# The last down group of the feed-forward parts: four column tiles instead of two, gone through token tile by token tile

## Chip, cores and metric

One core of a Trainium2 chip runs the whole program once. The metric is the device time of that execution in microseconds (us). Before the change the median of three runs is 1692.49 us (1692.39 to 1693.67).

## What is computed

Two layers of a block with 256 latent tokens (x) and 256 context tokens (ctx), 1024 wide. Each layer is: a feed-forward part, a mixer (two kinds of attention and a short convolution), a second feed-forward part. The last layer's second feed-forward part is made for the 256 latent tokens only, since only they are returned.

```python
def swiglu(u, wi, wo):
    g, up = jnp.split(u @ wi, 2, axis=-1)      # wi: 1024 x 5632
    return (jax.nn.silu(g) * up) @ wo          # wo: 2816 x 1024

h = post(h, swiglu(pre(h, m, 0, 0), ffn_wi[0], ffn_wo[0]), m, 0, 1, 0.5)
```

`pre` is an RMS norm with a scale and a shift per column, `post` adds the gated, normed result to the residual stream h. So there are four feed-forward parts: parts 1 (layer 0, first), 2 (layer 0, second) and 3 (layer 1, first) over 512 tokens, part 4 (layer 1, second) over 256.

## The kernel before

**Number format.** Every product of two matrices is made of three matmuls: both operands are split into a high and a low half (`a` and the weight slot `w` hold both; `Uh`/`Ul` are the halves of the normed tokens), and high x high, low x high and high x low are summed in PSUM. `mm` (line 79) issues them all, so the profile has one line for them; tiles and shapes tell them apart: `mm<-Uh,w` or `mm<-Ul,w` is an up matmul, `mm<-w,a` a down matmul, `mm<-w,Uh` one of a stage that goes token tile by token tile. The name ahead of the arrow (`at`, `mm`, `pv`) is only the PSUM bank's: six banks are handed out in the turn at, mm, at, mm, pv, mm.

**Weights.** `load_unit` (lines 86 to 95) brings one unit of 512 KB by DMA on the SP queue into a staging tile (two of them, three more in part 4), ScalarE casts it to the high half (line 93), VectorE subtracts to get the low half (line 94). A ring of eight slots holds the units. A slot is free again when the last matmul that reads it is done.

**A feed-forward part** (`ffn`). The 2816 inner columns are 22 column tiles f. `up` makes, for each f of a list, the gate and the up product (2 x 8 x 3 = 48 matmuls over the tokens of a segment), then `silu` (line 314, ScalarE), the product (315, VectorE), the high half (320, ScalarE) and the low half (321, VectorE) of `a[f]`. `down` multiplies a group of column tiles with wo: for each (t, hf) of a list of parts, t a token tile of 128 and hf a half of the 1024 output columns, 3 matmuls per f, all summed in one bank, which VectorE then adds to `y` (line 367; ScalarE copies the first group). `FGROUPS` says which column tiles are a group; ups are made one group ahead.

**The end of a part.** After the last group each (t, hf) has its sum of squares (line 208, ScalarE) and its gate product (370, VectorE); when hf is 1, `post(t)` makes the inverse root on GpSimd (line 99) and adds to H (274, VectorE, twice 512), and `after(t)` runs `pre(t)` for the next stage: two sums of squares of H (208), again an inverse root (104, 99), the scaled row `xn` (220, ScalarE), eight transposes on TensorE (225), scale and shift into `uf` (239 ScalarE, 241 VectorE), and the halves into the columns of tile t of `Uh` and `Ul` (243 ScalarE, 244 VectorE). `Uh`, `Ul`, `xn` and `uf` exist once. In part 4 `after` is the store.

The token order is t = 2, 3, 0, 1. In parts 1 to 3 the end is in pieces: the up of tiles 20 and 21 is made over tokens 256 to 511 before the down of group (16, 4), and over tokens 0 to 255 only after token tiles 2 and 3 have had their last down:

```python
down(20, 2, wu, [[(2, 0), (2, 1)], [(3, 0), (3, 1)]], False, True)
up([20, 21], wup, [(0, 8, 0, 256)], 0, 256)
down(20, 2, wu, [[(t, hf) for t in (0, 1) for hf in range(2)]], False, True)
```

so that the pre of tiles 2 and 3 runs beside the second up. The stage that follows begins with tile 2: the mixer (`token_block(2)`, after parts 1 and 3) and `up_first` of part 3 (after part 2) take eight units for tile 2, four and four, 24 matmuls of 512 columns for each four (in the mixer of the last layer the second 24 have 128 columns for tiles 2 and 3).

**Order.** Each engine's order of instructions is fixed ahead by a planner that plays the program with modelled times and takes what is ready, earlier work in the program first. Steps of the modulation vectors (`ada_step`, lines 151 to 164: one unit by DMA, then one or two multiply-reduces of 1024 on VectorE, line 162, whose product goes into `uf`) are hung behind the evictions of f = 3 to 19.

Of the kernel before, what the change touches and what calls it, by code (L numbers as in the profile page):

```python
# [16 lines left out]

D = 1024
NF = 22
FGROUPS = [(0, 4), (4, 4), (8, 4), (12, 4), (16, 4), (20, 2)]  # L20
EPS = 1e-6
NEG = -1e30

# [2 lines left out]
def tile_hybrid_block(ctx: ExitStack, tc: tile.TileContext, xin, c2, crow, w_ada, w_ada0, bcol, gcol, win, qkg, bias_in,  # L26
# [51 lines left out]
    def mm(out, lhsT, rhs, first, last):  # L78
        pe.matmul(out, lhsT=lhsT, rhs=rhs, start=first, stop=last)  # L79
# [6 lines left out]
    def load_unit(src):  # L86
        if more_stg:
            s = more_stg[0].tile([128, 1024], F32, name="stgx", tag="stgx", bufs=3)
        else:
            s = stg.tile([128, 1024], F32, name="stg", tag="stg")  # L90
        sp.dma_start(out=s, in_=src)
        w = next_slot()
        act.copy(w[:, 0], s)  # L93
        dve.tensor_tensor(out=w[:, 1], in0=s, in1=w[:, 0].bitcast(F32), op=ALU.subtract)  # L94
        return w
# [97 lines left out]
    def ada_to(ph, n):  # L193
        while ada_done[0] < min(n, len(ada_todo)):
            ada_todo[ada_done[0]](ph)
            ada_done[0] += 1

    def load_gate(l, mi, nv):
        G = work.tile([128, 2, 1024], F32, name="G", tag="G")
        dr = gates.pop(9 * l + mi)  # L200
        pool.dma_start(out=G[:, 0:nv].rearrange("p v c -> p (v c)"),
                       in_=bass.AP(tensor=dr.tensor, offset=dr.offset, ap=[[0, 128], [1, 1024 * nv]]))
        return G

    def sumsq(src, n):
        j = work.tile([128, 1024], BF16, name="junk", tag="junk")
        ss = small.tile([128, 1], F32, name="ss", tag="ss", bufs=12)
        act.activation(j[:, 0:n], src, AF.Square, accum_out=ss)  # L208
        return ss
# [60 lines left out]
    def post(t, yg, ss0, ss1):  # L270
        r = rsum(sum_eps(ss0, ss1))
        for i, y in enumerate(yg):
            h = H[t][:, 512 * i:512 * i + 512]
            dve.scalar_tensor_tensor(out=h, in0=y, scalar=r, in1=h, op0=ALU.mult, op1=ALU.add)
# [14 lines left out]
    def ffn(ph, l, i, U, tiles, after, ada_target, mode):  # L289
# [6 lines left out]
        def load_up(fs):  # L296
            return {(f, u): load_unit(wi[l, i, f, u]) for f in fs for u in range(2)}

        def up(fs, ws, segs, c0, n):
            pss = {(f, u): cur["mm"]() for f in fs for u in range(2)}  # L300
            for k0, nk, s0, sn in segs:
                for f in fs:
                    for u in range(2):
                        w = ws[f, u]
                        po = pss[f, u][:, s0 - c0:s0 - c0 + sn]
                        for kt in range(k0, k0 + nk):
                            wh = w[:, 0, 128 * kt:128 * kt + 128]
                            wl = w[:, 1, 128 * kt:128 * kt + 128]
                            mm(po, wh, U[0][:, kt, s0:s0 + sn], kt == 0, False)
                            mm(po, wh, U[1][:, kt, s0:s0 + sn], False, False)  # L310
                            mm(po, wl, U[0][:, kt, s0:s0 + sn], False, kt == 7)
            for f in fs:
                sg = ph.tile([128, 512], F32, name="sg", tag="sg")
                act.activation(sg[:, 0:n], pss[f, 0][:, 0:n], AF.Silu)
                dve.tensor_tensor(out=sg[:, 0:n], in0=pss[f, 1][:, 0:n], in1=sg[:, 0:n], op=ALU.mult)  # L315
                if f not in acts:
                    acts[f] = ph.tile([128, 2, n_c], F32R, name="a", tag="a", bufs=6)
                a = acts[f]
                c = slice(c0 - lo_c, c0 - lo_c + n)
                act.copy(a[:, 0, c], sg[:, 0:n])  # L320
                ins = dve.tensor_tensor(out=a[:, 1, c], in0=sg[:, 0:n], in1=a[:, 0, c].bitcast(F32), op=ALU.subtract)
                if f == 10:
                    n0 = len(nc.cur_bb.bb.instructions)
                    G.append(load_gate(l, mi, 1 if len(tiles) == 2 else 2))
                    tc.add_manual_dep(nc.cur_bb.bb.instructions[n0], ins.ins.name,
                                      mybir.DependencyInfo(mybir.DependencyClass.NoSync, mybir.DependencyReason.DATA),
                                      reason="gate late")
                if c0 == lo_c and 3 <= f < 20:
                    with tc.issue_after(ins.ins):
                        ada_to(ph, ada0 + (ada_target - ada0) * (f - 2) // 17)  # L330

        def up_all(fs, mode=""):
            if mode == "k":
                segs = [(2 * qd, 2, lo_c, n_c) for qd in range(4)]
            elif mode[0:3] == "tok":
                segs = [(0, 8, 256, 256), (0, 8, 0, 256)]
            else:
                segs = [(0, 8, lo_c, n_c)]
            up(fs, load_up(fs), segs, lo_c, n_c)

        def load_down(f0, nf, hf):
            return [load_unit(wo[l, i, (f0 + fp) // 2, hf]) for fp in range(0, nf, 2)]

        def down(f0, nf, wu, parts, first, last):
            for part in parts:
                ps = {x: cur["mm"]() for x in part}
                for f in range(nf):
                    for t, hf in part:
                        if hf not in wu:
                            wu[hf] = load_down(f0, nf, hf)  # L350
                        p = ps[t, hf]
                        c = 128 * t - lo_c
                        ah, al = acts[f0 + f][:, 0, c:c + 128], acts[f0 + f][:, 1, c:c + 128]
                        wh = wu[hf][f // 2][:, 0, 512 * (f % 2):512 * (f % 2) + 512]
                        wl = wu[hf][f // 2][:, 1, 512 * (f % 2):512 * (f % 2) + 512]
                        mm(p, ah, wh, f == 0, False)
                        mm(p, al, wh, False, False)
                        mm(p, ah, wl, False, f == nf - 1)
                for t, hf in part:
                    p = ps[t, hf]  # L360
                    if t not in ys:
                        ys[t] = ph.tile([128, 1024], F32, name="y", tag="y", bufs=len(tiles))
                    y = ys[t][:, 512 * hf:512 * hf + 512]
                    if first:
                        act.copy(y, p)
                    else:
                        dve.tensor_tensor(out=y, in0=p, in1=y, op=ALU.add)  # L367
                    if last:
                        sss[t, hf] = sumsq(y, 512)
                        dve.tensor_tensor(out=y, in0=y, in1=G[0][:, 0 if t < 2 else 1, 512 * hf:512 * hf + 512], op=ALU.mult)  # L370
                        if hf == 1:
                            post(t, [ys[t][:, 0:512], ys[t][:, 512:1024]], sss[t, 0], sss[t, 1])
                            after(t)
# [23 lines left out]
        else:  # L397
            up_all([0, 1, 2], mode)
            up_all([3])
        for g, (f0, nf) in enumerate(FGROUPS[:-1]):  # L400
            f1 = f0 + nf
            if f1 < 20:
                up_all([f1, f1 + 1])
            elif len(tiles) == 4:
                wup = load_up([20, 21])
                up([20, 21], wup, [(0, 8, 256, 256)], 256, 256)
            else:
                up_all([20, 21])
            down(f0, nf, {}, [[(t, hf)] for hf in range(2) for t in tiles], g == 0, False)
            if f1 < 20:  # L410
                up_all([f1 + 2, f1 + 3])
        wu = {}
        if len(tiles) == 4:
            down(20, 2, wu, [[(2, 0), (2, 1)], [(3, 0), (3, 1)]], False, True)
            up([20, 21], wup, [(0, 8, 0, 256)], 0, 256)
            down(20, 2, wu, [[(t, hf) for t in (0, 1) for hf in range(2)]], False, True)
        else:
            down(20, 2, wu, [[(t, hf)] for t in tiles for hf in range(2)], False, True)

    def mixer(ph, l, U, after):  # L420
        full = l == 0
# [278 lines left out]
    with phase("ffn") as ph:  # L700
        ffn(ph, 0, 0, U, order, after, 54, "k")
# [4 lines left out]
    with phase("ffn") as ph:  # L706
        ffn(ph, 0, 1, box2[0], order, after, 90, "tok1")
    box2, after = chain(1, 1)
    with phase("ffn") as ph:
        ffn(ph, 1, 0, box[0], order, after, 144, "tok2")  # L710
# [83 lines left out]
```

## Time and profile before

| | |
|---|---|
| median of three runs | 1692.49 us (1692.39 to 1693.67) |
| the profiled execution | 1692.87 us |
| its span (first to last instruction) | 1691.0 us |
| mean granted TensorE clock over the span | 0.997 |
| busy: TensorE matmul / weight load / VectorE / ScalarE / GpSimd | 98% / 83% / 68% / 43% / 3% |
| moved by DMA | 259.98 MB, mean 154 GB/s |

The profile is of one execution. It lies 0.38 us above the median of the runs, and 1.87 us of it are outside the span. PE is TensorE's matmuls, PEld its weight loads, DVE VectorE, ACT ScalarE, POOL GpSimd, SPq the queue that issues most DMAs. Since matmuls are pipelined, the duration of one is longer than the step from one to the next; steps are read from the starts or from the chain of waits, which lists each instruction with the time by which it carries the chain on.

### The profile page before, as it was taken

To read this page: it belongs to the slowest core of one execution; us is meant where nothing else is said; L and a number is where in the kernel's file an instruction comes from. 1 tells how busy PE (TensorE), PEld (TensorE's weight loads), DVE (VectorE), ACT (ScalarE), POOL (GpSimd) and SP (SyncE) were. 2 spreads that over 40 slices of the span, in tenths; PEclk is the share of its full clock that TensorE was granted. 3 is DMA by queue.
4 is the path that set the end of the run, shared out by engine and by line. 5 is a ranking of instruction groups with operands and counts; after the bars stand their busy time and mean duration, and the time that the engine had idled before them with its cause. 6 is when DMAs were issued, how large, how long until landed. Compare 5 with 4: busy or idle time off the path is not lost.

```text
span 1691.0 us, 23323 instructions
## 1 busy us (share of the span) xinstructions
PE 1662.5 (98%) x9012; PEld 1406.9 (83%) x9012; DVE 1146.9 (68%) x1917; ACT 720.4 (43%) x1247; POOL 46.9 (3%) x77
## 2 busy tenths in 40 slices
PE   6999999999999999999999999999999999999997
PEld 4888888888887789888888888888888889879997
DVE  3578787667766665476675566887785768865654
ACT  5432222227656683322222364322222557865442
POOL 1000000001100010000000000000000020000000
PEclk9999999999999999999999999999999999999999
DMA  8565555432121334454444134665563322456551
GB/s 322 200 226 197 174 200 189 160 112 106 63 75 51 94 125 162 149 193 145 161 163 148 64 137 155 216 204 189 167 215 125 106 94 101 138 172 215 181 193 64
DMA packets 73503, 259.98 MB, mean 154 GB/s; under 512 B 8440, under 2 KB 11728, under 8 KB 72496
## 3 DMA queue, kind: packets, MB, share of 16 engines
q1 hardware_dynamic: 72144, 252.81, 43.9%
q0 software_dynamic: 1248, 5.68, 1.0%
q8 instruction: 71, 1.16, 0.3%
q14 instruction: 40, 0.33, 0.1%
HBM read 257.37 MB, written 1.09 MB: 153 GB/s over the span
## 4 chain that ended last, share of the span: by engine, by line
PE 96%; DVE 1%; ACT 1%; DMA 1%; issue 0%; SPq 0%; POOL 0%; DVEq 0%; POOLq 0%; ACTq 0%
PE mm L79 52%; PE at L79 27%; PE pv L79 14%; PE ptr L590 2%; PE ptr L225 1%; DMA H<-in_xin_dram 0%; ACT junk L208 0%; DMA stg<-in_wi_tm_dram 0%; ACT w L93 0%; DMA bias<-in_bias_dram 0%; ACT xn L220 0%; DVE y L370 0%; DVE w L94 0%; PE ptr L469 0%; DVE y L367 0%
## 5 line engine op out<-in xcount | busy, mean ns | idle before, releaser
L79 PE MATMUL mm<-Uh,w 128*128 128x512 f32 (+1 forms) x1808 | 486.2, 348 | 0.0
L93 ACT CAST w<-stg 128x1024 fp32r<-128x1024 f32 x262 | 274.7, 1051 | 442.9 <-PE mm L79 392.2
L94 DVE TENSOR_TENSOR w<-stg,w 128x1024 fp32r<-128x1024 f32 x262 | 319.6, 1222 | 163.5 <-ACT w L93 162.5
L79 PEld LDWEIGHTS mm<-Uh,w 128*128 128x128 f32 x1808 | 319.2, 189 | 42.8 <-issue 0.6
L79 PE MATMUL mm<-Ul,w 128*128 128x512 f32 (+1 forms) x904 | 314.5, 348 | 0.0
L162 DVE CUSTOM_DVE_ANT_0 uf<-adas,CB 128x1024 f32<-128x1024 f32 x248 | 302.7, 1221 | 14.9 <-DMA adas<-in_w_ada_dram 11.1
L79 PE MATMUL at<-Uh,w 128*128 128x512 f32 (+1 forms) x960 | 254.1, 344 | 0.0
L79 PE MATMUL mm<-w,a 128*128 128x512 f32 x924 | 226.7, 389 | 0.0
L79 PEld LDWEIGHTS mm<-w,a 128*128 128x128 f32 x924 | 173.4, 188 | 35.9
L79 PEld LDWEIGHTS mm<-Ul,w 128*128 128x128 f32 x904 | 171.2, 189 | 21.1 <-issue 0.2
L79 PEld LDWEIGHTS at<-Uh,w 128*128 128x128 f32 x960 | 169.0, 190 | 22.0 <-issue 0.4
L79 PE MATMUL mm<-w,Uh 128*128 128x512 f32 (+1 forms) x544 | 171.1, 387 | 0.4 <-ACT w L93 0.4
L79 PE MATMUL at<-Ul,w 128*128 128x512 f32 (+1 forms) x480 | 165.4, 345 | 0.4 <-DVE Ul L267 0.4
L79 PE MATMUL at<-w,a 128*128 128x512 f32 x594 | 146.8, 390 | 0.9 <-ACT a L320 0.9
L79 PEld LDWEIGHTS at<-w,a 128*128 128x128 f32 x594 | 111.0, 188 | 24.3 <-ACT a L320 1.8
L79 PE MATMUL pv<-Uh,w 128*128 128x512 f32 (+1 forms) x464 | 127.6, 353 | 0.0
L79 PEld LDWEIGHTS mm<-w,Uh 128*128 128x128 f32 x544 | 100.4, 188 | 19.6 <-ACT w L93 0.7
L315 DVE TENSOR_TENSOR sg<-mm,sg 128x512 f32<-128x512 f32 (+1 forms) x86 | 51.3, 597 | 90.9 <-PE mm L79 85.0
L94 DVE TENSOR_TENSOR w<-stgx,w 128x1024 fp32r<-128x1024 f32 x58 | 71.0, 1224 | 52.5 <-ACT w L93 52.3
L79 PE MATMUL mm<-w,Ul 128*128 128x512 f32 (+1 forms) x272 | 105.2, 387 | 0.0
L79 PEld LDWEIGHTS at<-Ul,w 128*128 128x128 f32 x480 | 91.1, 190 | 11.8 <-DVE Ul L267 1.0
L79 PEld LDWEIGHTS pv<-Uh,w 128*128 128x128 f32 x464 | 82.7, 189 | 12.0
(161 smaller groups left out, 1709.8 us busy)
## 6 DMA issues: line engine op xcount, KB each, us to landing
adas<-in_w_ada_dram SPq DMA_DIRECT2D x144, 512.0 KB, 3.4
stg<-in_wi_dram SPq DMA_DIRECT2D x124, 512.0 KB, 4.0
stg<-in_wo_dram SPq DMA_DIRECT2D x66, 512.0 KB, 3.3
stg<-in_win_dram SPq DMA_DIRECT2D x40, 512.0 KB, 3.3
stgx<-in_wi_dram SPq DMA_DIRECT2D x36, 512.0 KB, 4.2
stgx<-in_wo_dram SPq DMA_DIRECT2D x22, 512.0 KB, 4.3
stg<-in_woa_dram SPq DMA_DIRECT2D x16, 512.0 KB, 3.3
stg<-in_wi_tm_dram SPq DMA_DIRECT2D x16, 512.0 KB, 3.3
```

The lines of the kernel that those rows point to most:

```text
L79: pe.matmul(out, lhsT=lhsT, rhs=rhs, start=first, stop=last)
L93: act.copy(w[:, 0], s)
L94: dve.tensor_tensor(out=w[:, 1], in0=s, in1=w[:, 0].bitcast(F32), op=ALU.subtract)
L162: dve.tensor_tensor_reduce(out=junk, in0=s, in1=CB[:, v], op0=ALU.mult, op1=ALU.add, scale=1.0, scalar=0.0, accum_out=ada_mc[m][:, v, cb:c ...
L225: pe.transpose(pt[:, b], xn[:, 128 * k:128 * k + 128], I)
L315: dve.tensor_tensor(out=sg[:, 0:n], in0=pss[f, 1][:, 0:n], in1=sg[:, 0:n], op=ALU.mult)
L590: pe.transpose(pt[:, b], P[:, 128 * b:128 * b + 128], I)
```

## The change

The groups become five of 4, 4, 4, 4, 2 and a last one of 4. The up of tiles 20 and 21 is made over all tokens, the last group (tiles 18 to 21) is gone through by token tile, and within one by half: (2,0), (2,1), (3,0), (3,1), (0,0), (0,1), (1,0), (1,1), or in part 4 (0,0), (0,1), (1,0), (1,1). The sequence at the end becomes: up 18, 19; down of group (16, 2); up 20, 21; down of group (18, 4).

```diff
-FGROUPS = [(0, 4), (4, 4), (8, 4), (12, 4), (16, 4), (20, 2)]
+FGROUPS = [(0, 4), (4, 4), (8, 4), (12, 4), (16, 2), (18, 4)]
...
         for g, (f0, nf) in enumerate(FGROUPS[:-1]):
             f1 = f0 + nf
-            if f1 < 20:
-                up_all([f1, f1 + 1])
-            elif len(tiles) == 4:
-                wup = load_up([20, 21])
-                up([20, 21], wup, [(0, 8, 256, 256)], 256, 256)
-            else:
-                up_all([20, 21])
+            up_all([f1, f1 + 1])
             down(f0, nf, {}, [[(t, hf)] for hf in range(2) for t in tiles], g == 0, False)
-            if f1 < 20:
+            if FGROUPS[g + 1][1] == 4:
                 up_all([f1 + 2, f1 + 3])
-        wu = {}
-        if len(tiles) == 4:
-            down(20, 2, wu, [[(2, 0), (2, 1)], [(3, 0), (3, 1)]], False, True)
-            up([20, 21], wup, [(0, 8, 0, 256)], 0, 256)
-            down(20, 2, wu, [[(t, hf) for t in (0, 1) for hf in range(2)]], False, True)
-        else:
-            down(20, 2, wu, [[(t, hf)] for t in tiles for hf in range(2)], False, True)
+        down(18, 4, {}, [[(t, hf)] for t in tiles for hf in range(2)], False, True)
```

## Rows read from the trace of the kernel before

**Rows 1.** The page: busy us (share of the span) xinstructions; chain of waits by engine.

```profile
PE 1662.5 (98%) x9012; PEld 1406.9 (83%) x9012; DVE 1146.9 (68%) x1917; ACT 720.4 (43%) x1247; POOL 46.9 (3%) x77
...
PE 96%; DVE 1%; ACT 1%; DMA 1%; issue 0%; SPq 0%; POOL 0%; DVEq 0%; POOLq 0%; ACTq 0%
```

**Rows 2.** PE's waits over the span: us in total, times, longest us.

```profile
PE ptr L225 <- ACT xn L220: 12.1, 4, 10.2
```

**Rows 3.** The chain of waits, end of part 1: start us, us, what.

```profile
334.86 5.44 PE mm L79 x24
340.30 2.87 PE at L79 x24
...
348.93 2.88 PE mm L79 x24
...
379.04 2.87 PE pv L79 x24
...
387.67 2.88 PE mm L79 x24
```

**Rows 4.** PE's waits in 978 to 981 us, then in 1348 to 1375 us.

```profile
PE at L79 <- ACT a L320: 0.9, 1, 0.9
...
PE ptr L225 <- ACT xn L220: 0.8, 1, 0.8
```

**Rows 5.** The timeline of PE, ACT and DVE, end of part 4: start us, us.

```profile
1680.81 1.52 PE L79 MATMUL mm<-w,a 128*128 128x512 f32 x6
...
1682.36 0.69 DVE L367 TENSOR_TENSOR y<-mm,y 128x512 f32<-128x512 f32 x1
...
1683.69 0.19 ACT L208 ACTIVATION_READ_ACCUMULATOR junk<-y 128x1 f32 x1
...
1683.57 1.41 DVE L274 SCALAR_TENSOR_TENSOR H<-y,rr,H 128x512 f32<-128x512 f32 x2
1684.89 0.68 DVE L370 TENSOR_TENSOR y<-y,G 128x512 f32<-128x512 f32 x1
1685.50 0.21 DVE L104 TENSOR_SCALAR sst<-ss 128x1 f32<-128x1 f32 x1
```

**Rows 6.** The page's groups: the modulation steps on VectorE.

```profile
L162 DVE CUSTOM_DVE_ANT_0 uf<-adas,CB 128x1024 f32<-128x1024 f32 x248 | 302.7, 1221 | 14.9 <-DMA adas<-in_w_ada_dram 11.1
```

**Rows 7.** The timeline, PE, ACT and DVE: eviction of a 512-token column tile, part 1.

```profile
329.25 0.39 PE L79 MATMUL pv<-Uh,w 128*128 128x512 f32 x1
...
329.45 1.06 ACT L93 CAST w<-stg 128x1024 fp32r<-128x1024 f32 x1 [3.90 <-PE mm L79]
330.41 0.62 ACT L320 CAST a<-sg 128x512 fp32r<-128x512 f32 x1
...
331.68 0.68 DVE L321 TENSOR_TENSOR a<-sg,a 128x512 fp32r<-128x512 f32 x1
```

**Rows 8.** The timeline, PE, ACT and DVE: tile 2's end, part 1, then part 2.

```profile
376.15 0.84 PE L79 MATMUL at<-w,a 128*128 128x512 f32 x3
...
386.70 1.15 ACT L220 ACTIVATE xn<-H,rr 128x1024 f32<-128x1024 f32 x1
387.91 1.05 ACT L93 CAST w<-stg 128x1024 fp32r<-128x1024 f32 x1
...
391.09 1.03 PE L225 MATMUL ptr<-I,xn 128*128 128x128 f32 x8
...
394.54 1.29 DVE L244 TENSOR_TENSOR Ul<-uf,Uh 128x512 fp32r<-128x512 f32 x2
...
960.27 0.84 PE L79 MATMUL at<-w,a 128*128 128x512 f32 x3
...
979.71 1.29 DVE L244 TENSOR_TENSOR Ul<-uf,Uh 128x512 fp32r<-128x512 f32 x2
```

**Rows 9.** ACT's timeline after part 1; the page's DMA issues (median us to landing).

```profile
398.41 1.04 ACT L93 CAST w<-stg 128x1024 fp32r<-128x1024 f32 x1
...
stg<-in_wi_tm_dram SPq DMA_DIRECT2D x16, 512.0 KB, 3.3
```

## The prediction, made before the changed kernel was run

> **What bounds the kernel now.** I read the page's busy times and chain first: PE is busy for 98% of the span and carries 96% of the chain of waits [rows 1]. Then PE's waits: the largest kind is 12.1 us, of which one wait at the start is 10.2 [rows 2]. So almost all the time is matmul steps issued back to back. The change can win by fewer or shorter matmul steps and by waits of PE that go, and it can lose by new waits of PE. VectorE (68%) and ScalarE (43%) [rows 1] count only where PE waits for them. I then read the ends of the four feed-forward parts, the only places that the change touches.
>
> **The split up is joined.** In the chain, a group of 24 up matmuls over 512 tokens takes 5.44 us (0.2267 a matmul), one over 256 tokens 2.88 (0.1200) [rows 3]. At the end of parts 1 to 3 the up of tiles 20 and 21 stands as four groups of 256 (the first at 340.30, the last at 348.93), and four more after the last down of tiles 2 and 3 (379.04 to 387.67) [rows 3]. That is 8 x 2.88 = 23.04 us. After the change the same product is four groups of 512, 4 x 5.44 = 21.76. Gain: 1.28 us in each of three parts, **-3.84 us**, all on PE's own chain. The number of down matmuls stays (22 tiles x 3 per token tile and half), and so do the bank adds (six groups before and after) and the weight units.
>
> A pair of half matmuls costs 2 x 0.1200 - 0.2267 = 13.3 ns more than one whole [rows 3]. [...] The sum goes by the rows.
>
> **Old waits that go.** In part 2 PE waits 0.9 us for the high half of a tile-20 or -21 `a` [rows 4], since its eviction stands in ScalarE's and VectorE's queues among the pre of tiles 2 and 3. After the change no pre has begun when tile 21 is evicted: **-0.9**. In the last mixer PE waits 0.8 for `xn` of a late token tile [rows 4]. Before, tiles 0 and 1 finish together at the end of the down; after, tile 0 has finished 2 x 2.72 = 5.44 us earlier (2.72 is 12 x 0.2267): **-0.8**.
>
> **The end of the program.** The last matmul ends at 1680.81 + 1.52 = 1682.33 and the span at 1691.0. VectorE carries that tail: it adds the last bank at 1682.36, makes tile 0's H first (1683.57, 1.41 us), and only then tile 1's last gate product (1684.89) and its sum (1685.50) [rows 5]. After the change a part of part 4's last group lasts 2.72 us instead of 1.36, tile 0's H is done before tile 1's bank is full, and the gate product need only wait for its sum of squares, done at 1683.69 + 0.19 = 1683.88 [rows 5]. With a hop it starts at 1683.95 instead of 1684.89: **-0.95**. If the sum is placed ahead of the gate product it is 1.6, the far end.
>
> **New: tile 21 is needed soon after its up.** The first part (2, 0) has 9 matmuls on tiles 18 to 20 (2.04 us), then tile 21's high half, and 0.23 later its low half. After an up group of 512 that ends at 329.25 the trace has the high half at 330.41 + 0.62 = 331.03 and the low one at 331.68 + 0.68 = 332.36, so 1.8 and 3.1 us after, because the freed slot's next unit is cast in between (329.45, 1.06 us) [rows 7]. 3.1 against 2.27: 0.85 us of wait a part if PE keeps the written order, none where the planner puts matmuls of (2, 1) in between, which have a bank. I take about half, **+1.2** for three parts; ends 0 and 2.6. Part 4's evictions are over 256 tokens, shorter: nothing.
>
> **New: tile 2 has less time.** Its last matmul is now followed by six parts of 2.72 = 16.3 us and its own eight transposes (0.87), 17.2 us, until PE wants its `Uh`. Before, its chain from the last matmul (376.15) to `Ul` (394.54 + 1.29) took 19.7 us, in part 2 20.7 [rows 8]; there 5.44 + 11.52 + 5.44 less 2.72 = 19.7 us stood behind it, so it was just in time. But 3.2 us of it is `xn` waiting for its place in PE's order (386.70 + 1.15 to 391.09), and four casts of new weight units stand in it (387.91 is one, 1.05 each) [rows 8]. After the change only one unit is cast in that stretch until hf 0's slots come free, and (2, 0) has been added and squared 2.72 us earlier. I lay the chain out again with the rows' durations and tile 3's evictions between: `xn` ends about 8 us and `Ul` 13 to 15 us after the last matmul. Taken: **+0.5** in all; ends 0 and (2.5 + 3.5 + 2.5) = 8.5, if the chain stays as long as before. Tile 3 then has a further tile's matmuls of the next stage before it is needed, and nothing waits.
>
> **New: later slots for the next stage.** Before, six of the next stage's eight units are converted by the end of the down, the last two right after (398.41) [rows 9]. After, four slots come free with the up of 20 and 21, two 2.72 us before the end, and two at the end, while one DMA lands in 3.3 us [rows 9] and a staging tile is only free once VectorE is through. Units 7 and 8: -2.72 + 1.05 + 1.22 + 3.3 to 4.3 + 1.05 + 1.22 is 5.1 to 6.1 us after the end, a unit later 7.4. After parts 1 and 2 they are wanted at 8.2 and 9.5, in the last mixer at about 6 to 7. Uncontended it just fits; VectorE is behind with tiles 0 and 1. Taken **+0.7**, ends 0 and 2.5. The DMAs keep their order on SP; none is added.
>
> **At nothing:** the down of (16, 2) makes a bank full each 1.36 us and VectorE needs 0.69 for its add [rows 5], beside modulation steps of 1.22 [rows 6]. Six banks give 8.2 us of slack; without that cover each delayed add would stop PE for up to 1.22. Waiting adds hold back the conversions behind them on VectorE, which have the 21.8 us up of 20 and 21 before they are missed.
>
> **Sum:** -3.84 - 0.9 - 0.8 - 0.95 + 1.2 + 0.5 + 0.7 = -4.1 us. Against the profiled execution's 1692.87 that is 1688.8; it lies 0.38 above the median, so against 1692.49: **1688.4 us**. A measurement of this kernel can tell about 0.2%, 3.4 us, from no change: faster is below 1689.1, slower above 1695.9.
>
> **The rivals.**
> 1. *The new waits eat it.* The waits for tile 21 and for units 7 and 8 come at their far ends (2.6 and 2.5): -6.5 + 2.6 + 0.5 + 2.5 = -0.9, 1691.6. For it: the eviction pattern of rows 7 is regular. Against: the planner has so far filled such holes (PE hardly waits). 0.22.
> 2. *Slower: tile 2 becomes the wall.* The place is the first matmul of the next stage; it decides from 17.2 us of chain on. With the chains of rows 8 as they are: -6.5 + 1.2 + 0.7 + 8.5 = +3.9, 1696.4, since PE has no other work there. For it: both chains shown are longer than 17.2, and VectorE has about 7 us of work per token tile at a pace of 5.44 (two adds, two gate products, H, two sums [rows 5], `Ul` at 1.29 [rows 8], a scale and shift I put at as much). Against: the four casts and the place in PE's order that lengthen them go. 0.13.
> 3. [...] 0.03.
> 4. *The change does more than it says:* the planner lays the whole program anew and moves waits in stages not edited. The size can only be guessed from the waits that its order leaves now: of the largest kind 1.9 us beside the one at the start [rows 2], so say up to 3 either way, 1685.4 or 1691.4. 0.06.
>
> **How the numbers follow.** The forecast has 0.56; its own range is 1686.0 (no new wait) to 1690.0, of which 0.44 lies below 1689.1 and 0.12 above. Faster: 0.44 + 0.04 (rival 4) = 0.48. Same: 0.12 + 0.22 + 0.03 + 0.01 = 0.38. Slower: 0.13 + 0.01 = 0.14. The range goes from 1685.8, just under the sum without new waits, to 1695.0, past rivals 1 and 3 and into the milder part of 2; about 0.06 lies below and 0.11 above.
>
> **What would show it.** Right: the groups of 24 x 2.88 of tiles 20 and 21 are gone and four of 5.44 stand there; PE's waits at the four ends stay under 1 us each; the tail after the last matmul shrinks from 8.7 to about 7.7 us. Wrong: PE waits for `Uh`, `Ul` or `xn` at the start of the next stage (rival 2), for `a` in (2, 0) or for `w` in the next stage (rival 1), or waits appear in the attention stages (rival 4).

## The result, and the profile after

The changed kernel takes 1706.45 us (median of 4 runs, 1703.79 to 1706.90), the kernel before 1692.44 in the same session: a ratio of 1.0081 with an interval of 1.0067 to 1.0095. It is slower by 14.0 us, where 4 us less were forecast, and lies outside the range. The profiled execution took 1703.79 us with a span of 1702.0 (before 1692.87 and 1691.0), so the rows below tell of 11.0 of the 14.0 us; its mean granted clock is 0.994, in the three other runs 0.992 to 0.993.

The page of after: busy times, and the chain of waits by engine, as in [rows 1].

```profile
PE 1663.1 (98%) x8724; PEld 1393.4 (82%) x8724; DVE 1145.1 (67%) x1905; ACT 717.8 (42%) x1235; POOL 48.5 (3%) x77
...
PE 94%; DVE 2%; DMA 1%; ACT 1%; issue 1%; POOL 0%; SPq 0%; DVEq 0%; POOLq 0%; ACTq 0%
```

PE has 288 matmuls fewer (3 x 96, the halves that were joined) and is no less busy. PE's share of the chain falls from 96% to 94%, and VectorE's rises from 1% to 2%. Something has put VectorE on the path.

PE's waits of after over the span (us in total, times, longest us), as in [rows 2]:

```profile
PE ptr L225 <- ACT xn L220: 19.6, 7, 11.4
```

The longest of them, 11.4 us, is the one at the start of the program (10.2 before). It doesn't add to the loss: some 30 us later the same matmul starts 0.5 us earlier than before (39.55 against 40.01). And in 318 to 440 us alone, the end of part 1:

```profile
PE ptr L225 <- ACT xn L220: 2.3, 1, 2.3
PE mm L79 <- DVE Ul L244: 1.3, 1, 1.3
PE mm L79 <- ACT Uh L243: 0.4, 1, 0.4
```

That is 4.0 us of new waits at the end of part 1. Part 2 has 2.3 for `xn` and 1.0 for `Ul`, part 3 2.3, 1.1 and 0.4: 4.0 + 3.3 + 3.8 = 11.1 us in the three ends. The end of part 4 has none of this kind. No wait for `a` and none for `w` of a next stage came.

The chain of waits of after, end of part 1 (start us, us, what), as in [rows 3]:

```profile
350.76 5.44 PE at L79 x24
356.20 5.44 PE mm L79 x24
361.64 5.44 PE pv L79 x24
367.08 5.44 PE mm L79 x24
372.52 2.04 PE at L79 x9
374.56 2.04 PE mm L79 x9
376.60 2.27 PE at L79 x10
```

The joined up of tiles 20 and 21 stands as forecast: four groups of 5.44 and none of 2.88. Behind it the parts (2, 0), (2, 1) and (3, 0) stand with 9, 9 and 10 matmuls, each cut off before its last two or three.

The timeline of after around that place, sorted by what follows from what, PE, DVE and ACT (start us, us; in brackets the wait before it). It answers to [rows 7] and [rows 8]:

```profile
374.79 0.69 DVE L321 TENSOR_TENSOR a<-sg,a 128x512 fp32r<-128x512 f32 x1
...
376.44 2.43 PE L79 MATMUL at<-w,a 128*128 128x512 f32 x10
...
380.29 0.62 PE L79 MATMUL mm<-w,a 128*128 128x512 f32 x2
...
381.10 0.68 DVE L367 TENSOR_TENSOR y<-mm,y 128x512 f32<-128x512 f32 x1
...
388.20 1.14 ACT L220 ACTIVATE xn<-H,rr 128x1024 f32<-128x1024 f32 x1
...
391.39 2.44 PE L79 MATMUL mm<-w,a 128*128 128x512 f32 x10
393.67 1.03 PE L225 MATMUL ptr<-I,xn 128*128 128x128 f32 x8
394.46 0.70 PE L79 MATMUL mm<-w,a 128*128 128x512 f32 x2
397.46 1.09 PE L225 MATMUL ptr<-I,xn 128*128 128x128 f32 x8 [2.31 <-ACT xn L220]
398.92 0.73 PE L79 MATMUL mm<-w,Uh 128*128 128x512 f32 x2 [0.36 <-ACT Uh L243]
...
396.26 1.15 ACT L220 ACTIVATE xn<-H,rr 128x1024 f32<-128x1024 f32 x1
397.30 1.05 ACT L93 CAST w<-stg 128x1024 fp32r<-128x1024 f32 x1
398.23 1.15 ACT L243 CAST Uh<-uf 128x512 fp32r<-128x512 f32 x2
...
400.20 1.28 DVE L244 TENSOR_TENSOR Ul<-uf,Uh 128x512 fp32r<-128x512 f32 x2
```

Read it in four steps.

- **The hole.** Tile 21's low half is done at 374.79 + 0.69 = 375.48, 3.0 us after the up ends at 372.52. PE doesn't wait for it: matmuls of (2, 1) and (3, 0) on tiles 18 to 20 are placed in between, and go on to 378.7. Only then come the last steps of (2, 0) and (2, 1). Tile 2's last matmul ends at 380.29 + 0.62 = 380.91, and its last bank is added at 381.10.
- **The cover.** The ten matmuls of (3, 0) that were to run behind tile 2's end have run ahead of it. The down ends at 394.46 + 0.70 = 395.16, so what stands behind tile 2 is 14.3 us long, not the 17.2 of the forecast.
- **The place.** `xn` of tile 2 is done at 389.34, and its eight transposes stand in PE's order at 393.67, 4.3 us later, behind ten matmuls of (1, 1).
- **The last leg.** From the transposes' end (394.70) to the end of `Ul` (401.48) it takes 6.8 us: on ScalarE `xn` of tile 3 and a cast come before `Uh`, and PE itself stands 2.31 us at tile 3's transposes, which have been placed ahead of the next stage's first matmul.

From tile 2's last matmul to `Ul` that makes 20.6 us, against 14.3 of cover.

### The profile page after: what moved, and what is told of

Same layout as the page of the kernel before. It is cut to its first block, busy times and chain, and to the rows that moved or that the text cites. A ratio compares the mean times of both kernels' runs of the same rounds, so it can differ in the third digit from the quotient of the medians.

```text
span 1702.0 us, 22709 instructions
## 1 busy us (share of the span) xinstructions
PE 1663.1 (98%) x8724; PEld 1393.4 (82%) x8724; DVE 1145.1 (67%) x1905; ACT 717.8 (42%) x1235; POOL 48.5 (3%) x77
## 4 chain that ended last, share of the span: by engine, by line
PE 94%; DVE 2%; DMA 1%; ACT 1%; issue 1%; POOL 0%; SPq 0%; DVEq 0%; POOLq 0%; ACTq 0%
PE mm L79 51%; PE at L79 26%; PE pv L79 14%; PE ptr L578 2%; DMA adas<-in_w_ada_dram 1%; PE ptr L225 1%; ACT junk L208 0%; DVE w L94 0%; DMA H<-in_xin_dram 0%; DVE y L370 0%; DVE H L274 0%; DVE y L367 0%; ACT w L93 0%; DMA bias<-in_bias_dram 0%; DVE uf L241 0%
## 5 line engine op out<-in xcount | busy, mean ns | idle before, releaser
L79 PEld LDWEIGHTS mm<-Uh,w 128*128 128x128 f32 x1712 | 306.1, 189 | 46.4 <-issue 0.6
L162 DVE CUSTOM_DVE_ANT_0 uf<-adas,CB 128x1024 f32<-128x1024 f32 x248 | 302.9, 1221 | 14.0 <-DMA adas<-in_w_ada_dram 10.2
L79 PE MATMUL mm<-Ul,w 128*128 128x512 f32 (+1 forms) x856 | 305.8, 357 | 0.0
L79 PE MATMUL at<-Uh,w 128*128 128x512 f32 (+1 forms) x864 | 242.0, 357 | 0.0
L79 PEld LDWEIGHTS mm<-Ul,w 128*128 128x128 f32 x856 | 161.7, 189 | 23.2 <-issue 0.2
L79 PEld LDWEIGHTS at<-Uh,w 128*128 128x128 f32 x864 | 154.8, 189 | 23.7 <-ACT w L93 0.2
L79 PE MATMUL at<-w,a 128*128 128x512 f32 x636 | 155.5, 389 | 0.0
L79 PE MATMUL at<-Ul,w 128*128 128x512 f32 (+1 forms) x432 | 154.3, 357 | 0.0
L79 PEld LDWEIGHTS at<-w,a 128*128 128x128 f32 x636 | 119.1, 188 | 24.5
L79 PE MATMUL pv<-Uh,w 128*128 128x512 f32 (+1 forms) x464 | 133.7, 364 | 0.0
L79 PEld LDWEIGHTS at<-Ul,w 128*128 128x128 f32 x432 | 81.8, 189 | 12.2 <-DVE Ul L267 0.4
```

The source lines that it names most:

```text
L162: dve.tensor_tensor_reduce(out=junk, in0=s, in1=CB[:, v], op0=ALU.mult, op1=ALU.add, scale=1.0, scalar=0.0, accum_out=ada_mc[m][:, v, cb:c ...
```

## The experiments

The leading theory after this reading (called "tile 21" in the expectations) is that the hole for tile 21 delays tile 2's end. The rivals: tile 2's chain is too long even with tile 2 in time ("cover"), the order in which the planner places the pieces, the weight slots, and the granted clock. A and B in the two expectations on the transposes' place are each that experiment's own. Kernels that ran in one session share the runs of the kernel before, and each ratio is against these. The kernel before has a median of 1692.44 us in the session of the result and 1694.04, 1693.48 and 1693.49 in the three others, so the difference of two medians from different sessions is uncertain by up to 1.6 us; where such a difference is given, the one by the ratios stands beside it.

**The split put back, the rest of the change kept.**

```diff
-            if FGROUPS[g + 1][1] == 4:
-                up_all([f1 + 2, f1 + 3])
-        down(18, 4, {}, [[(t, hf)] for t in tiles for hf in range(2)], False, True)
+            if f1 < 18:
+                if FGROUPS[g + 1][1] == 4:
+                    up_all([f1 + 2, f1 + 3])
+        if len(tiles) == 4:
+            wu = {}
+            wup = load_up([20, 21])
+            up([20, 21], wup, [(0, 8, 256, 256)], 256, 256)
+            down(18, 4, wu, [[(2, 0), (2, 1)], [(3, 0), (3, 1)]], False, True)
+            up([20, 21], wup, [(0, 8, 0, 256)], 0, 256)
+            down(18, 4, wu, [[(t, hf) for t in (0, 1) for hf in range(2)]], False, True)
...
```

> The changed kernel with the split up put back in parts 1 to 3 (last group still four tiles, part 4 untouched). Theory cover (the new time is PE waiting at the start of the next stage for tile 2's pre, because the up half of 11.5 us no longer stands behind it): the waits of 2.3 + 0.4 + 1.3 us go in all three parts and the time comes to 1692 to 1695 us. Rival tile 21 (the time comes from the last group of four wanting tile 21 right after its up, which holds back tile 2's banks): that order is still there, so the time stays at 1700 us or more. Rival slots (eight slots are held by four up and four down units, so the next stage's units are late): PE waits for w at the start of the next stage, 2 to 4 us a part, 1699 to 1704 us.

Measured: 1692.79 us (1692.02 to 1694.16), ratio 0.9992 (0.9983 to 1.0001). Of the new waits only 0.6 us for `Uh` in part 3 is left. That is what "cover" expected, and not the 1700 or more of "tile 21". Here too matmuls of tile 3 are placed ahead of tile 2's last ones on tile 21 (368.05 to 369.58 in part 1), but the down goes on to 397.84, and with 28.3 us behind tile 2 the delay costs nothing. So the groups of two and four in themselves cost nothing that can be measured; the loss belongs to joining the up, which takes away what stood behind tile 2's end.

**The up joined alone**, in the kernel before, with its last group of two made token tile by token tile. Tile 2 then has only six parts of half the length behind it.

```diff
-            elif len(tiles) == 4:
-                wup = load_up([20, 21])
-                up([20, 21], wup, [(0, 8, 256, 256)], 256, 256)
             else:
                 up_all([20, 21])
...
-            down(20, 2, wu, [[(2, 0), (2, 1)], [(3, 0), (3, 1)]], False, True)
-            up([20, 21], wup, [(0, 8, 0, 256)], 0, 256)
-            down(20, 2, wu, [[(t, hf) for t in (0, 1) for hf in range(2)]], False, True)
...
+        down(20, 2, {}, [[(t, hf)] for t in tiles for hf in range(2)], False, True)
```

> The kernel before with the up of tiles 20 and 21 joined in parts 1 to 3 and its last group still of two tiles, token tile by token tile. Behind tile 2 stand six parts of 1.36 us = 8.2 us, half of the changed kernel's 16.3. Theory cover: the wait at the end of each of the three parts is some 8 us longer than in the changed kernel, 24 us in all: 1722 to 1734 us. Rival tile 21: here the down of tiles 16 to 19 stands between that up and the last down, nothing wants tile 21 early, so the time is below the changed kernel's, 1696 to 1702 us.

Measured: 1712.49 us (1710.96 to 1713.81), ratio 1.0108 (1.0092 to 1.0123), between the two expectations. The waits are 2.5 for `xn`, 1.7 to 1.8 for `Uh` and 0.8 to 1.1 for `Ul` in each part. With half as long parts behind tile 2 the time is worse by another 6 us than in the changed kernel (4.6 by the ratios), but far from what "cover" expected of it: in part 1 the chain takes 16.1 us here, from tile 2's last matmul (385.51 + 1.52 = 387.03) to the end of `Ul` (401.85 + 1.28 = 403.13), and not 20.6. So it is not of a fixed length. That it is shorter because less other work stands in it is an argument and was not tested. Without a hole it still is a little longer than the 13 to 15 us of the forecast.

**The down of tiles 16 and 17 behind the up of tiles 20 and 21**, so that tile 21 is long done when its first matmul comes. Nothing else in the changed kernel is touched.

```diff
             up_all([f1, f1 + 1])
+            if f1 == 18:
+                up_all([20, 21])
             down(f0, nf, {}, [[(t, hf)] for hf in range(2) for t in tiles], g == 0, False)
-            if FGROUPS[g + 1][1] == 4:
+            if f1 < 18 and FGROUPS[g + 1][1] == 4:
                 up_all([f1 + 2, f1 + 3])
```

> The changed kernel with the down of group (16, 2) moved behind the up of tiles 20 and 21, so that tile 21 is ready when the last group begins. Theory tile 21: tile 2's banks are full 5.4 us after the last group's start instead of 7.9, the waits at the start of the next stage shrink by about 2.4 us in each of three parts, part 4's tail by 1.7, and with shorter waits the granted clock stays at 1.0: 1693 to 1698 us. Theory cover alone (the fill costs nothing, only the 16.3 us behind tile 2 count): 1703 to 1706 us, as the changed kernel.

Measured: 1694.47 us (1692.48 to 1695.38), ratio 0.9999 (0.9990 to 1.0009). It takes 12.0 us off the changed kernel (13.9 by the ratios), as "tile 21" expected. Its timeline at the end of part 1, PE, DVE and ACT:

```profile
375.38 2.88 PE L79 MATMUL mm<-w,a 128*128 128x512 f32 x12
...
378.30 0.69 DVE L367 TENSOR_TENSOR y<-mm,y 128x512 f32<-128x512 f32 x1 [0.55 <-PE mm L79]
...
385.36 1.14 ACT L220 ACTIVATE xn<-H,rr 128x1024 f32<-128x1024 f32 x1
...
390.80 1.03 PE L225 MATMUL ptr<-I,xn 128*128 128x128 f32 x8
...
398.68 0.50 PE L79 MATMUL mm<-w,Ul 128*128 128x512 f32 x1 [1.86 <-DVE Ul L244]
...
397.94 1.28 DVE L244 TENSOR_TENSOR Ul<-uf,Uh 128x512 fp32r<-128x512 f32 x2
```

Tile 2's last bank is added at 378.30 instead of 381.10, 2.8 us earlier, and all that hangs on it moves up by about as much (`xn` 385.36 instead of 388.20, transposes 390.80 instead of 393.67). The waits for `xn` and `Uh` are gone; one of 1.9 to 2.0 us for `Ul` stays in each part. So, with the up joined, the filled hole is the larger part of the loss, and what is left, 5.8 us of waits, just eats the gain. What is left speaks for "cover": from tile 2's last matmul (375.38 + 2.88 = 378.26) to the end of `Ul` (397.94 + 1.28 = 399.22) the chain takes 21.0 us, though nothing is late, and the down goes on to 395.47, which is the 17.2 us of the forecast.

**The adds to H and the pre of each token tile raised in priority**, the changed kernel otherwise.

```diff
                         if hf == 1:
+                          with tc.high_priority():
                             post(t, [ys[t][:, 0:512], ys[t][:, 512:1024]], sss[t, 0], sss[t, 1])
```

> The changed kernel with post and pre of every token tile marked as urgent for the planner, nothing else. Theory order (tile 2's chain is long because casts of later weight units and tile 3's steps are planned ahead of its halves, and its transposes 4.3 us after xn): the wait at the start of the next stage falls by 2 to 4 us a part, 1694 to 1700 us. Theory cover or tile 21 alone: the chain of dependent steps itself is too long, gain under 1 us a part, 1702 to 1706 us.

Measured: 1705.05 us (1702.47 to 1706.13), ratio 1.0062 (1.0047 to 1.0077), not to be told from the changed kernel. Tile 2's transposes stay 4.4 us behind `xn` (389.25 + 1.14 to 394.74), and a cast of a weight unit still stands between `xn` of tile 3 and `Uh`. The edit hardly moved the order, so it says little about what the order is worth.

**The transposes' place in PE's order set by hand:** in parts 1 to 3 of the changed kernel the matmuls of (1, 1) may not stand ahead of tile 2's transposes. A dependency is added that orders the two on PE and waits for nothing.

```diff
-                pe.transpose(pt[:, b], xn[:, 128 * k:128 * k + 128], I)
+                last_ptr[t] = pe.transpose(pt[:, b], xn[:, 128 * k:128 * k + 128], I)
...
-                        mm(p, ah, wh, f == 0, False)
+                        m = mm(p, ah, wh, f == 0, False)
+                        if last and len(tiles) == 4 and (t, hf) == (1, 1) and f == 0:
+                            tc.add_manual_dep(m.ins, last_ptr[2].ins.name,
+                                              mybir.DependencyInfo(mybir.DependencyClass.NoSync,
+                                                                   mybir.DependencyReason.DATA), reason="place")
```

> The changed kernel with one thing more: in parts 1 to 3 the last down part (1, 1) may not stand ahead of tile 2's eight transposes in PE's order, so they come about 2.3 us earlier behind tile 2's xn, and tile 3's transposes fall behind tile 2's first 24 matmuls of the next stage; the time at which tile 2's last bank is full stays as it is. Theory A (part of the loss is the place that the order gives the transposes): the waits of 2.3 for xn go, those for Uh and Ul shrink from 0.4 and 1.3 to at most 0.5 together per part, the granted clock stays at 1.00 there; 3 x (2.3 + 0.4 + 1.3 - 0.5) = 10.5 us less at the most, of which xn coming late may leave some: 1693 to 1698 us. Theory B (the place is harmless, the chain on VectorE and ScalarE from tile 2's late end is the wall): PE waits as long as before, only at tile 2's own transposes or at Uh: 1702 to 1706 us.

Measured: 1699.08 us (1696.42 to 1700.76), ratio 1.0036 (1.0022 to 1.0050): between the two. PE's timeline at the end of part 1:

```profile
391.84 1.03 PE L227 MATMUL ptr<-I,xn 128*128 128x128 f32 x8
392.63 2.98 PE L79 MATMUL mm<-w,a 128*128 128x512 f32 x12
396.99 0.73 PE L79 MATMUL mm<-w,Uh 128*128 128x512 f32 x2 [1.38 <-ACT Uh L245]
398.57 0.50 PE L79 MATMUL mm<-w,Ul 128*128 128x512 f32 x1 [0.85 <-DVE Ul L246]
```

The transposes come 1.8 us earlier with tile 2's end as late as before, and the 2.3 us for `xn` are gone in all three ends (in the last mixer a wait of 0.9 for the `xn` of a later token tile is back, much as in [rows 4]). What stays is 1.4 for `Uh` and 0.9 to 1.1 for `Ul` in each part, where theory A allowed 0.5 together. So the place of the transposes, tile 3's with them, is worth 7.4 us of the 14.0 (7.6 by the ratios), the clock that comes back with it counted in (it reads 1.00 from 980 to 1000 and from 1345 to 1370, where the changed kernel has 0.83 and 0.86); the rest is tile 2's late end and its last leg. This doesn't add up with the 12.0 of the moved down: both edits take from the same waits.

**Both together**, the kernel with the down of tiles 16 and 17 moved, and the transposes bound to stand ahead of (1, 0): the same edit as the last with `(1, 0)` for `(1, 1)`.

> The kernel in which the down of tiles 16 and 17 stands behind the up of 20 and 21 (as in e3_ups_first), with tile 2's transposes ahead of part (1, 0) in PE's order instead of behind it. In e3_ups_first xn was ready at 386.5 in part 1 and its transposes stood at 390.8, with 1.9 us of wait for Ul left per part. Theory A (the place is the last of what makes tile 2 late): the transposes come 2 us earlier, the waits for Ul of 1.9 per part fall to under 0.3, 3 x 1.6 = 4.8 us less: 1688 to 1691 us. Theory B (Ul is held by VectorE's other work, or tile 3 and the weight units take the waits over): Ul's waits stay above 1 us per part: 1692.5 to 1695.5 us.

Measured: 1693.59 us (1691.85 to 1695.50), ratio 1.0001 (0.9992 to 1.0010): theory B's time. But the edit didn't do what it was made for. Other matmuls were placed ahead of the transposes instead of those of (1, 0), and they start at 390.82, where they started at 390.80 without it. It says nothing on their place. It does show what `Ul` waits for, once more. VectorE's timeline, end of part 1:

```profile
393.03 1.36 DVE L243 TENSOR_SCALAR uf<-ptr,GP,COLS 128x128 f32<-128x128 f32 x4
394.31 1.40 DVE L276 SCALAR_TENSOR_TENSOR H<-y,rr,H 128x512 f32<-128x512 f32 x2
395.64 0.68 DVE L373 TENSOR_TENSOR y<-at,y 128x512 f32<-128x512 f32 x1
396.24 1.21 DVE L94 TENSOR_TENSOR w<-stg,w 128x1024 fp32r<-128x1024 f32 x1
...
397.97 1.28 DVE L246 TENSOR_TENSOR Ul<-uf,Uh 128x512 fp32r<-128x512 f32 x2
```

Between tile 2's `uf` and its `Ul` VectorE makes tile 0's H, two bank adds and a weight unit, without a gap, and PE waits behind them. That VectorE's order is what holds `Ul` here is read from this row of work; no kernel with that order changed was run.

**PE kept busy.** In the profiled execution of after the granted clock falls behind the waits of parts 2 and 3. The view by windows: its bounds and length in us, the busy time of PE, PEld, DVE, ACT and POOL with their instructions, the granted clock, the share of the DMA engines, GB/s:

```profile
980.00:985.00 5.00, 2.56 (x18) 1.73 (x16) 4.87 (x12) 4.97 (x12) 1.48 (x2) 0.92 0.57 204
985.00:990.00 5.00, 4.00 (x9) 2.72 (x10) 5.00 (x10) 4.94 (x13) 0.55 (x1) 0.50 0.34 116
990.00:992.00 2.00, 2.00 (x8) 1.62 (x7) 1.55 (x4) 2.00 (x5) 0.31 (x1) 0.74 1.03 297
992.00:996.00 4.00, 4.00 (x22) 3.35 (x21) 2.83 (x5) 1.98 (x6) 0.94 (x3) 1.00 0.90 333
...
1356.00:1358.00 2.00, 1.05 (x4) 0.50 (x2) 2.00 (x4) 2.00 (x4) 0.00 (x0) 0.57 0.00 0
1358.00:1362.00 4.00, 3.47 (x8) 2.82 (x9) 4.00 (x9) 3.94 (x13) 0.55 (x1) 0.50 0.57 192
1362.00:1364.00 2.00, 2.00 (x11) 1.64 (x10) 1.31 (x4) 2.00 (x4) 0.86 (x2) 0.73 1.00 332
```

In the second stretch, where the granted clock reads 0.50, nine matmuls keep PE busy for 4.00 us. To test what that costs, ten matmuls over 512 columns, whose bank nothing reads, were put behind the last down of parts 1 to 3 of the changed kernel. They run while PE would wait.

```diff
         down(18, 4, {}, [[(t, hf)] for t in tiles for hf in range(2)], False, True)
+        if len(tiles) == 4:
+            p = cur["mm"]()
+            for x in range(10):
+                mm(p, acts[21][:, 0, 0:128], acts[21][:, 0], x == 0, x == 9)
```

> The changed kernel with ten matmuls of 512 columns whose sum nobody reads, behind the last down of parts 1 to 3, where PE stands idle for 2.3 us. They take no time of their own if they fit there. Theory clock (part of the loss is that after such a wait the granted clock falls to half for some 6 us in two or three of the parts): the granted clock stays at 1.0 through those stretches, 1698 to 1702 us, and the runs agree more closely. Rival (the clock is a by-product, the waits are the whole loss): no change, 1704 to 1707 us.

Measured: 1702.89 us (1702.41 to 1703.31), ratio 1.0054 (1.0042 to 1.0067). PE's timeline in it, then two windows of it (the same columns as above):

```profile
396.37 2.45 PE L79 MATMUL at<-a 128*128 128x512 f32 x10
```

```profile
980.00:1000.00 20.00, 18.12 (x83) 14.34 (x82) 15.75 (x31) 16.32 (x38) 3.65 (x6) 0.91 0.65 226
1345.00:1370.00 25.00, 23.15 (x125) 19.24 (x124) 23.09 (x46) 22.31 (x50) 6.29 (x12) 1.00 0.40 127
```

The fillers take the place of the wait for `xn` (396.37 + 2.45 = 398.82), nothing comes earlier by them, and still the kernel is 3.6 us faster by the medians than without them (4.6 by the ratios), between the two expectations; the two ratios' intervals just touch. In the same two windows the changed kernel has a clock of 0.83 and 0.86, this one 0.91 and 1.00. So, as an estimate from these two kernels, about 3.6 of the 14.0 us are the clock, and as part 2 still shows a dip (0.91), that is rather a lower bound. The spans of the two profiled executions differ by less, 1702.0 and 1700.9: this one comes to the last group of part 1, where no filler has run yet, 1.4 us later (373.72 against 372.36), and its other waits at the three ends make 5.5 us where the changed kernel has 4.2.

**The change in part 4 alone.**

```diff
+        if len(tiles) == 2:
+            groups = [(0, 4), (4, 4), (8, 4), (12, 4), (16, 2), (18, 4)]
+            for g, (f0, nf) in enumerate(groups[:-1]):
...
+            down(18, 4, {}, [[(t, hf)] for t in tiles for hf in range(2)], False, True)
+            return
```

> The kernel before with the change made in part 4 alone. There no stage follows, PE's matmul time is the same and only the tail differs. Theory tile 21: the first banks of the last group fill late (all at once after tile 21's eviction), tile 0's H stands in VectorE's queue ahead of the last bank's add, and the tail after the last matmul is 9.3 us against 8.7: 1692.5 to 1694 us. My blind reading (the gate product moves forward): 0.9 us shorter, 1691 to 1692 us.

Measured: 1694.42 us (1692.32 to 1694.90), ratio 1.0003 (0.9994 to 1.0012). In size it can't be told from no change. Its trace has the tail of the changed kernel: the last matmul ends at 1680.58 + 2.88 = 1683.46 and the span at 1692.7, so 9.2 us, where before it was 8.7 and 7.7 had been forecast; "tile 21" had 9.3.

**A last group of six.** If the hole and the short cover are the whole loss, a group that gives tile 2 more behind it and has tile 21 done in time must bring the gain that was forecast. Tiles 16 to 21 are all made first, and the last group takes six column tiles, token tile by token tile: six parts of 18 matmuls behind tile 2.

```diff
-FGROUPS = [(0, 4), (4, 4), (8, 4), (12, 4), (16, 2), (18, 4)]
+FGROUPS = [(0, 4), (4, 4), (8, 4), (12, 4), (16, 6)]
...
-            if FGROUPS[g + 1][1] == 4:
-                up_all([f1 + 2, f1 + 3])
-        down(18, 4, {}, [[(t, hf)] for t in tiles for hf in range(2)], False, True)
+            up_all([f1 + 2, f1 + 3])
+            if f1 == 16:
+                up_all([20, 21])
+        down(16, 6, {}, [[(t, hf)] for t in tiles for hf in range(2)], False, True)
```

> The up of tiles 20 and 21 joined as in the changed kernel, but the last group has six tiles (16 to 21), so behind tile 2 stand six parts of 4.08 = 24.5 us, and tile 21 is wanted 15 matmuls after its up. Five groups in all, one addition into y less per token tile. Theory cover: no wait for tile 2's halves at the start of the next stage, the joined up's 3.8 us are gained in full: 1687 to 1690 us. Rival slots: six units are held to the end, only two of the next stage's can be converted early, PE waits for w some 2 to 4 us a part: 1693 to 1701 us.

Measured: **1685.25 us** (1684.96 to 1685.48), ratio 0.9951 (0.9938 to 0.9963), a little under the 1687 to 1690 of "cover". It beats both kernels. PE's timeline at the end of part 1, then PE and DVE at the end of the program:

```profile
382.51 1.03 PE L225 MATMUL ptr<-I,xn 128*128 128x128 f32 x8
...
393.27 3.43 PE L79 MATMUL mm<-w,a 128*128 128x512 f32 x14
396.54 0.39 PE L79 MATMUL mm<-w,Uh 128*128 128x512 f32 x1
...
1671.22 4.24 PE L79 MATMUL mm<-w,a 128*128 128x512 f32 x18
...
1675.50 0.69 DVE L367 TENSOR_TENSOR y<-mm,y 128x512 f32<-128x512 f32 x1 [1.23 <-PE mm L79]
```

The hole for tile 21 is there too, but the first part has fifteen matmuls on other tiles ahead of it, and of (3, 0) only a single one is pulled forward; tile 2's last matmul ends at about 370.7. PE goes from the down into the next stage without a wait, in all three parts. The granted clock is 1.00 around the three ends, and the last matmul ends at 1671.22 + 4.24 = 1675.46, 7.7 us before the end of the span (1683.2): the shorter tail that was forecast. The last bank's add starts 0.04 us after it: nothing stands ahead of it on VectorE.

The experiments can be put in the order of what stands behind tile 2's last matmul in part 1. With 8.2 us of it (the up joined alone) PE waits 5.1 us at the start of the next stage, with 14.3 (the changed kernel) 4.0, with 17.2 (the down moved) 1.9; with the 19.7 of the kernel before, the 26.0 of the group of six and the 28.3 of the split put back it doesn't wait.

## Why the prediction was wrong

**What held.** The join: four groups of 5.44 a part and no pair of 2.88. A step of 512 columns still takes 5.44 / 24 = 0.2267 us, as in [rows 3], and 24 matmuls of 256 columns 2.88 us where a run still has them (at 376.53 in part 1 of the kernel with the split put back), so a pair of halves costs 13.3 ns more than one whole in the runs after the change too. For rival 3, a cheaper pair (the 0.03 in the chances, and a point of the range), no run shows a figure. The wait of 0.9 us for `a` in [rows 4] is gone and no wait for a weight unit came: the +0.7 for later slots measured 0. The adds of (16, 2) stopped PE nowhere.

**The step that failed: "New: tile 2 has less time", taken at +0.5.** It measured 11.1 us of waits and the clock behind them. Three things in its working were wrong.

1. The cover. 17.2 us came from the order in which the kernel is written. The step before it, "tile 21 is needed soon after its up", said that PE wouldn't wait where matmuls of (2, 1) are put in between, and costed this fill at nothing. The fill was placed, and PE didn't wait for tile 21; but the filling matmuls came from behind tile 2's end and put it back. With tile 21 early, the same bank was added 2.8 us earlier and the kernel was 12.0 us faster (13.9 by the ratios). The cost of that hole was rightly looked for and wrongly placed: not at the hole, but 20 us later.
2. The chain, laid out at 13 to 15 us, took 20.6, about as long as before. With tile 2 in time and the 17.2 us of cover that were forecast it took 21.0, and the three ends still waited 5.8 us: about half of the 11.1 would have come without the hole. The first leg was right (`xn` forecast 8 us after the last matmul, measured 389.34 - 380.91 = 8.4). The prediction took the wait of `xn` for its place in PE's order, 3.2 us in [rows 8], to go with the change. It was 4.3, and setting the place by hand gave 7.4 us back. The casts were to go too, all but one until the slots of half 0 come free; in the trace three weight units are cast ahead of `Uh`, at 390.23, 391.81 and 397.30. And the last leg was laid out with tile 3's evictions alone; in the trace it takes 6.8 us, with tile 3's `xn` and transposes, its H and weight units on both engines ahead of `Uh` and `Ul`. Before, the same leg took 3.7 us (391.09 + 1.03 to 394.54 + 1.29) [rows 8]. (The moments 329.25 and 376.15, which the prediction takes for ends, are the starts of the next matmul in [rows 7] and [rows 8]; the ends lie 0.2 us later, which changes nothing.)
3. The clock. No term had it: the mean granted clock of the profiled executions is 0.997 before and 0.994 after. [rows 1] show a PE that hardly ever waits, and the prediction read no row on what the clock does where it waits.

**The end of the program, -0.95, measured +0.6** (1702.0 - 1692.75 = 9.3 against 8.7). The timeline of after, PE and DVE, as in [rows 5]:

```profile
1689.87 2.88 PE L79 MATMUL mm<-w,a 128*128 128x512 f32 x12
...
1693.03 1.42 DVE L274 SCALAR_TENSOR_TENSOR H<-y,rr,H 128x512 f32<-128x512 f32 x2 [0.46 <-POOL rr L99]
1694.36 0.69 DVE L367 TENSOR_TENSOR y<-mm,y 128x512 f32<-128x512 f32 x1
```

The hole for tile 21 is filled here too, so tile 0's banks fill late, tile 0's H (1693.03) stands on VectorE ahead of the last bank's add, and the add starts at 1694.36, 1.6 us after the last matmul's end (1689.87 + 2.88 = 1692.75). "Part 4's evictions are over 256 tokens, shorter: nothing" was the step. They are shorter (the low half takes 0.42 us against 0.68, in both kernels); the last bank was late all the same. The 0.07 us that the prediction put between a sum of squares and the gate product was its author's estimate; in after the last gate product starts 0.03 us behind its sum (1695.68 + 0.19 = 1695.87, then 1695.90). With tile 21 in time the tail is as forecast: 7.7 in the kernel with the down moved (1683.30 to 1691.0), and 7.7 with the group of six.

**The rivals.** Rival 2, that tile 2 becomes the wall, is what happened, at the place that it named, and with the sign that the prediction gave for it: waits for `xn`, `Uh` and `Ul` at the start of the next stage. It had a chance of 0.13 and a price of 8.5 us; the waits made 11.1. The two arguments against it, that casts and the place in PE's order would go, were the ones that fell; its "for", that both chains shown in [rows 8] are longer than the cover, was the row to go by. Rival 1 had the right cause, tile 21, with the wrong effect.

**The account** of the profiled execution, all against the kernel before: +11.1 waits at the three ends, -3.84 join, -0.9 and -0.8 old waits, +0.6 tail come to +6.2. The span grew by 11.0. The clock can make up the 4.8 that are missing, by an estimate from the windows above: PE's busy time times what the clock lacks of 1.00 is 2.56 x 0.08 + 4.00 x 0.50 + 2.00 x 0.26 = 2.7 us in part 2, and 1.05 x 0.43 + 3.47 x 0.50 + 2.00 x 0.27 = 2.7 us in part 3, together 0.6 more than is missing. The starts of the same matmuls in both traces show where the time goes: after is 0.4 us ahead up to the end of part 1, 2.8 behind after it, 1.5 behind after the first mixer, 5.7 after the end of part 2, 10.2 after that of part 3 and 10.4 at the last matmul (1692.37 against 1681.94). So the three ends lose 3.2, 4.2 and 4.5 us, and the first mixer, which nobody edited, wins 1.4, the kind of thing that rival 4 named. That the other runs lie 2.3 to 3.1 us above the profiled one, at a lower mean clock, fits a third part falling too, but they have no trace; it was not shown. Of the 8.2 us that the group of six gains (1693.48 - 1685.25), 6.5 are the gains of the forecast; its fewer rounds of bank adds and smaller waits elsewhere may be the rest, which was not taken apart.

## What to carry to other kernels

When a stage's order is changed, write the chain that follows the stage against the work left behind it, with the longest chain that the trace shows and all the work that its engines have in that stretch; a delay that the order "fills" isn't gone if the filling work was the cover of something later. If an input arrives a few us late, make it earlier (here by moving one down behind one up) rather than let other work be pulled ahead. And the best kernel here is the one with the largest last group: the gain of the join was real, and it was kept where tile 2 was done some 26 us before the down's end (370.7 to 396.7), just eaten at 17 and more than eaten at 14.

## What the runs showed of the hardware

In the changed kernel the granted clock fell behind short waits of PE at two of the three ends: with waits of 3.3 us in part 2 and 3.8 in part 3 it read 0.50 for some us (in part 3 from 1358 to 1362), and the slower steps are estimated above at about 2.7 us each. After the wait of 2.3 us for `xn`, which ends at 983.47, the granted clock read 0.50 from 985 to 990 in part 2 of the changed kernel (the wait of 1.0 us for `Ul` falls into that stretch), with steps of 0.427 us (987.73 to 989.01 is three matmuls, 1.28 us) in place of 0.227, and 1.00 again from 992 to 996. In part 1, after a wait as long, it read 1.00 throughout (390 to 408), so one execution's trace doesn't tell whether a wait will cost that. The kernel whose last group is of six, without such waits, was also the steadiest: 1684.96 to 1685.48, against 1703.79 to 1706.90 in the changed one.
